# S5 preparation on GpSimd, its products on VectorE, and another order of the first block's stages

## The chip, the cores and the metric

The kernel runs on one core of one Trainium2 chip. Within the core TensorE (PE) multiplies matrices, VectorE (DVE), ScalarE (ACT) and GpSimd (POOL) work on tiles in SBUF and PSUM, and SyncE (SP) issues most of the loads. The metric is the device time of one execution in microseconds; lower is better.

## The reference

A first block (a mixer of two branches with a gate each, cross attention and a convolutional feed-forward layer) is followed by a second network of two further layers, on 256 tokens of 1024 channels. The change lies in the mixer of the first block:

```python
h = _rmsnorm(x, mix_norm_g[l])
u_s5, q_in, k_in, v_in, o_in, i_pre, f_pre, gate_pre = jnp.split(h @ w_in[l], split_points, axis=-1)
y_s5 = _s5(u_s5, ...)
y_m = _mlstm(q_in, k_in, v_in, o_in, i_pre, f_pre, ...)
g_s5, g_m = jnp.split(sigmoid(gate_pre + b_gate[l]), 2, axis=-1)
merged = g_s5 * (y_s5 @ w_br_s5[l]) + g_m * (y_m @ w_br_m[l])
x = x + merged @ w_out[l]
```

`_s5` is a linear recurrence with complex states, in 32 groups of 64 states and 16 channels:

```python
a_bar = jnp.exp(lam * dt)                       # dt = exp(log_dt)
b_bar = ((a_bar - 1.0) / lam)[..., None] * b_mat
_, states = lax.associative_scan(combine, (a_seq, bu), axis=1)
y = einsum(states, c_mat).real + d * u;  y = gelu(y);  y = y * sigmoid(y @ w_glu + b_glu)
```

`_mlstm` has a convolution of 4 taps over q and k (with SiLU), four heads with exponential gates over two chunks of 128 tokens, and a norm over each head.

## The kernel before

**Matrix products.** Weights come as fp32 tiles of 128 x 1024 (one DMA each, on SP) and are split into a high part (`hi`, L320, on ACT) and a rest (`lo`, L321, on DVE); `wload` makes both, and three matmuls (L328 to L330, or L337 to L339 with the tokens as rows) make one product step, with `xh` and `xl` the two parts of the activations. Three `hi` and three `lo` tiles exist in this block, so ACT and DVE run at most three weights ahead of PE. Two tiles of 128 x 1024 give one PSUM tile `g` of 128 x 512 (48 matmuls), called a pair below; `g` has three buffers, the smaller products (`a`) four.

**Order.** The program's text gives priorities (`high_priority`, and the order of writing), and the scheduler of the Tile framework sets each engine's own list from them by a simulated timeline. On the chip each engine works through its list strictly in order and waits at an instruction whose input isn't there.

**The first block's stages** as written: the S5 preparation `s5_prep`; the norm (`rms_defer`: squares, column sums at L454, the reciprocal root `rmsr` as a power on POOL at L505, a broadcast by PE at L498); `u` (two pairs, evacuated at L1637); `s5`, which makes everything from powers to the S5 output; `qk` (four pairs, each with its convolution `ev_qk`: a product with the token scale at L1646, six taps on DVE at L1654, and L1657); `vif`, `vm` and `o` (tokens as rows); `mlstm`; the eight gate pairs (L1696, L1698); `s5_glu`; the two branch products `w_brs` and `w_brm`; and the output projection `w_out`, where the block's mixer ends.

**S5 preparation.** `s5_prep` computes a_bar, its powers 0 to 4 (`pr`, `pi`), the input factors (`cr`, `ci`) and the scan factors (`akr`, `aki`, `akn`) from tiles of 128 x 16, in some hundred small instructions on DVE (a sine and cosine by polynomials among them); POOL computes two powers of e, `s5dt` and `s5er`. It has a high priority.

**S5 products.** For each of four blocks of four groups, `outer` multiplies factors and matrices: B on DVE (`mb`, 128 x 256, L747, then written into block diagonal form in two halves of the partitions, L759 and L762), C on POOL (`mc`, 128 x 320, L747, then L765 and L768 into `CR` and `CN`). PE transposes the B blocks (L772) and multiplies B with C (L777, L779) into the short kernel `KS`.

**State and scan.** 32 small matmuls (L795) make the chunk inputs, ACT copies them into `ST` (L796), and `combine` runs over `ST` ten times, five instructions each (L806 to L810). The S5 output (L830) multiplies `U`, `KS`, `ST`, `CR` and `CN`.

**mLSTM.** The gates' part (L859 to L899) is a chain of tiny instructions; each of four heads then does L905 on PE, `arg` (L908, DVE), exponentials on ACT, the scores (L914, L915), `pT` (L917, DVE), the sums (L919 to L921) and `hs` (L927, DVE). A norm over all heads follows (`rstd_cols`, a power on POOL), with `hn` (L937), a transposition (L938) and the branch's input.

Of the kernel before, what the change touches and what calls it, by code (L numbers as in the profile page):

```python
# [13 lines left out]
F32R = mybir.dt.float32r  # L14
# [6 lines left out]
P = 128  # L21
# [106 lines left out]
def host_arrays(i):  # L128
# [67 lines left out]
    pe_.add("lr", gp(g["s5_lam_re"][0]))  # L196
    pe_.add("li", gp(g["s5_lam_im"][0]))
# [61 lines left out]
def _program(ctx, tc, nc, a, offs, dump):  # L259
# [42 lines left out]
    def pexp(x, shape, tag):  # L302
# [5 lines left out]
        ts(c, x, ECOR, 1.0, op0=mult, op1=add)  # L308
        tt(r, r, c, op=mult)
        return r  # L310
# [328 lines left out]
    def s5_prep(bp):  # L639
        t16 = lambda tag, n=16: T(bp, [P, n], tag)  # L640
        lr, li, ldt = C["lr"], C["li"], C["ldt"]
        dt = pexp(ldt, [P, 16], "s5dt")
        xr, th = t16("xr"), t16("th")
        tt(xr, lr, dt, op=mult)
        tt(th, li, dt, op=mult)
        er = pexp(xr, [P, 16], "s5er")
# [10 lines left out]
        z, sn, cn, w = t16("z"), t16("sn"), t16("cn"), t16("w")  # L657
# [4 lines left out]
        stt(sn, sn, 1.0, r, op0=mult, op1=mult)  # L662
# [7 lines left out]
        j, cq, sq = t16("j"), t16("cq"), t16("sq")  # L670
        rnd(j, n, 0.25)
        stt(j, j, -4.0, n, op0=mult, op1=add)
        stt(w, j, -1.0, j, op0=mult, op1=ALU.max)
# [3 lines left out]
        pr = T(bp, [P, 16, 5], "pr")  # L677
        pi = T(bp, [P, 16, 5], "pi")
        G.memset(pr[:, :, 0:1], 1.0)
        G.memset(pi[:, :, 0:1], 0.0)  # L680
        ar, ai = pr[:, :, 1], pi[:, :, 1]

        def cmul(orr, oi, xr_, xi_, yr, yi):
            n_ = len(orr.shape) > 2 and orr.shape[2] or 1
            sh = list(orr.shape)
            t = [T(bp, sh, "cm%d_%d" % (n_, q_), bufs=2) for q_ in range(4)]
            tt(t[0], xr_, yr, op=mult)
            tt(t[1], xi_, yi, op=mult)
            tt(t[2], xr_, yi, op=mult)
            tt(t[3], xi_, yr, op=mult)  # L690
            tt(orr, t[0], t[1], op=sub)
            tt(oi, t[2], t[3], op=add)

        cs_, sn_ = t16("cs_"), t16("sn_")
        cmul(cs_, sn_, cn, sn, cq, sq)
        tt(ar, er, cs_, op=mult)
        tt(ai, er, sn_, op=mult)
        den, a1 = t16("den"), t16("a1")
        tt(den, lr, lr, op=mult)
        tt(z, li, li, op=mult)  # L700
        tt(den, den, z, op=add)
        V.reciprocal(den, den)
        nli = t16("nli")
        ts(nli, li, -1.0, None, op0=mult)
# [12 lines left out]
        akr, aki, akn = T(bp, [P, NL, 16], "akr"), T(bp, [P, NL, 16], "aki"), T(bp, [P, NL, 16], "akn")
        V.tensor_copy(akr[:, 0, :], pr[:, :, 4])
        V.tensor_copy(aki[:, 0, :], pi[:, :, 4])
        for k in range(1, NL):  # L720
            cmul(akr[:, k, :], aki[:, k, :], akr[:, k - 1, :], aki[:, k - 1, :], akr[:, k - 1, :], aki[:, k - 1, :])
        ts(akn, aki, -1.0, None, op0=mult)
        return cr, ci, pr, pi, akr, aki, akn

    def s5(bp, b2, K5, U, prep):
        cr, ci, pr, pi, akr, aki, akn = prep
        NL = 5
# [14 lines left out]
        def outer(eng, xa, ya, xb, yb, nt, tag):  # L742
            sh = [P, 4, nt, 16]
            m = []
            for x_, y_ in ((xa, ya), (xb, yb)):
                t = T(bp, sh, tag + str(len(m)))
                eng.tensor_tensor(t, bc(x_[:, :, :, None], sh), bc(y_[:, :, None, :], sh), op=mult)  # L747
                m.append(t)
            return m

        halves = [(g, slice(64 * g, 64 * g + 64)) for g in range(2)]
        for b in range(4):
            s4 = slice(4 * b, 4 * b + 4)
            BR, BI = bt[b % 2][:, 0], bt[b % 2][:, 1]
# [1045 lines left out]
```

## Time and profile before

| what | value |
|---|---|
| time, median of three runs | 1218.49 us (1217.42 to 1223.27) |
| the profiled execution | 1222.49 us, of which the span is 1220.7 |
| PE busy | 1175.4 us (96%) |
| DVE busy | 905.4 us (74%) |
| ACT busy | 681.7 us (56%) |
| POOL busy | 94.5 us (8%) |
| mean granted PE clock | 0.98 |

Busy shares are means over stages with different limits. A windows view gives each engine's busy time in a stretch, and PE's granted clock there (1.00 is 2.4 GHz, 0.50 is 1.2 GHz); a timeline gives each instruction's start and duration, and in square brackets how long its engine was idle before it and what ended that.

### The profile page before, as it was taken

What the parts mean: (1) busy time and instruction counts of PE and PEld (TensorE: products, weight loads), DVE (VectorE), ACT (ScalarE), POOL (GpSimd) and SP (SyncE); (2) the same over time, 40 slices, a digit from 0 to 9 for tenths busy, and PEclk for the clock granted to TensorE, in tenths of its full rate; (3) what the DMA queues carried; (4) which work ended last, traced back from release to release, by engine and by line L of the source; (5) the groups of instructions that cost most, each with busy time, mean ns of one, the idle gap of its engine ahead of it and who ended that gap; (6) DMA issues with size and microseconds to landing.
All of it is one profiled execution on the core that took longest, in us unless ns stands there. A gap on an engine that the chain in (4) does not pass through costs nothing.

```text
span 1220.7 us, 23603 instructions
## 1 busy us (share of the span) xinstructions
PE 1175.4 (96%) x9370; PEld 1111.6 (91%) x9370; DVE 905.4 (74%) x1744; ACT 681.7 (56%) x1205; POOL 94.5 (8%) x94
## 2 busy tenths in 40 slices
PE   7779999999999999999999899999999999999997
PEld 7769989999999999899998899998977789999986
DVE  8998957866689886667564886666687758976654
ACT  5345564755566765446355675554675566755541
POOL 4830000100000000000001000001000001000010
PEclk9979999999999999999999899999998999999998
DMA  7423445664356556656423556566754215666561
GB/s 262 139 87 114 147 137 179 205 202 157 100 177 196 183 177 181 196 175 215 163 79 106 170 173 187 176 181 190 261 182 139 70 54 193 208 188 188 160 201 36
DMA packets 61276, 199.41 MB, mean 163 GB/s; under 512 B 8502, under 2 KB 12398, under 8 KB 60910
## 3 DMA queue, kind: packets, MB, share of 16 engines
q1 hardware_dynamic: 54864, 191.60, 49.5%
q10 hardware_dynamic: 6302, 6.32, 1.6%
q8 instruction: 73, 1.20, 0.4%
q14 instruction: 37, 0.30, 0.1%
HBM read 196.28 MB, written 1.60 MB: 162 GB/s over the span
## 4 chain that ended last, share of the span: by engine, by line
PE 82%; DVE 11%; ACT 2%; DMA 2%; issue 2%; SPq 0%; DVEq 0%; ACTq 0%
PE g L329 10%; PE g L328 10%; PE g L330 10%; PE a L328 7%; PE a L329 7%; PE a L330 7%; PE a L393 5%; PE g L393 4%; DVE lo L321 3%; PE a L395 3%; PE g L337 2%; PE g L339 2%; PE g L338 2%; PE g L395 2%; PE a L947 1%
## 5 line engine op out<-in xcount | busy, mean ns | idle before, releaser
L321 DVE TENSOR_TENSOR lo<-raw,hi 128x1024 fp32r<-128x1024 f32 (+3 forms) x359 | 431.2, 1206 | 180.7 <-ACT hi L320 178.0
L320 ACT CAST hi<-raw 128x1024 fp32r<-128x1024 f32 (+3 forms) x359 | 363.7, 1020 | 355.4 <-PE g L329 138.8
L328 PE MATMUL g<-xh,hi 128*128 128x256 f32 (+1 forms) x616 | 176.2, 287 | 7.9 <-ACT xh L568 7.6
L329 PE MATMUL g<-xl,hi 128*128 128x256 f32 (+1 forms) x624 | 178.9, 287 | 0.3 <-DVE xl L569 0.3
L330 PE MATMUL g<-xh,lo 128*128 128x256 f32 (+1 forms) x616 | 176.3, 287 | 2.7 <-DVE lo L321 2.7
L328 PE MATMUL a<-nh,hi 128*128 128x256 f32 x560 | 159.9, 286 | 4.6 <-ACT sqa L1061 2.7
L329 PE MATMUL a<-nl,hi 128*128 128x256 f32 x560 | 159.5, 285 | 0.9 <-DVE nl L516 0.9
L330 PE MATMUL a<-nh,lo 128*128 128x256 f32 x560 | 159.3, 285 | 0.0
L328 PEld LDWEIGHTS g<-xh,hi 128*128 128x128 f32 x616 | 117.7, 191 | 9.9 <-ACT xh L568 7.9
L330 PEld LDWEIGHTS g<-xh,lo 128*128 128x128 f32 x616 | 117.4, 191 | 4.4 <-DVE lo L321 3.4
L329 PEld LDWEIGHTS g<-xl,hi 128*128 128x128 f32 x624 | 119.0, 191 | 1.4 <-DVE xl L569 0.9
L328 PEld LDWEIGHTS a<-nh,hi 128*128 128x128 f32 x560 | 108.6, 194 | 5.7 <-ACT sqa L1061 2.9
L329 PEld LDWEIGHTS a<-nl,hi 128*128 128x128 f32 x560 | 108.7, 194 | 1.1 <-DVE nl L516 1.1
L330 PEld LDWEIGHTS a<-nh,lo 128*128 128x128 f32 x560 | 108.7, 194 | 0.0
L393 PE MATMUL a<-mx,hi 128*128 128x512 f32 x264 | 91.9, 394 | 0.0
L328 PE MATMUL g<-nh,hi 128*128 128x256 f32 x288 | 81.5, 283 | 0.0
L329 PE MATMUL g<-nl,hi 128*128 128x256 f32 x288 | 81.5, 283 | 0.0
L330 PE MATMUL g<-nh,lo 128*128 128x256 f32 x288 | 81.5, 283 | 0.0
L395 PE MATMUL a<-mx,lo 128*128 128x256 f32 x264 | 73.1, 277 | 0.0
L393 PE MATMUL g<-mx,hi 128*128 128x512 f32 x198 | 69.0, 395 | 0.0
L393 PEld LDWEIGHTS a<-mx,hi 128*128 128x128 f32 x264 | 49.4, 188 | 11.5
L328 PEld LDWEIGHTS g<-nh,hi 128*128 128x128 f32 x288 | 55.3, 192 | 0.0
(619 smaller groups left out, 2905.2 us busy)
## 6 DMA issues: line engine op xcount, KB each, us to landing
raw<-g_up SPq DMA_DIRECT2D x88, 512.0 KB, 3.6
raw<-f_up SPq DMA_DIRECT2D x44, 512.0 KB, 3.5
raw<-g_dn SPq DMA_DIRECT2D x32, 512.0 KB, 3.6
raw<-w_fm SPq DMA_DIRECT2D x27, 512.0 KB, 4.1
raw<-ev_fm SPq DMA_DIRECT2D x20, 512.0 KB, 3.7
raw<-f_dn SPq DMA_DIRECT2D x16, 512.0 KB, 3.6
raw<-od_fm SPq DMA_DIRECT2D x14, 512.0 KB, 4.2
raw<-g_dn SPq DMA_DIRECT2D x16, 384.0 KB, 3.4
```

Of the source, the lines that this page charges most:

```text
L320: ACT.copy(hi, raw)
L321: tt(lo, raw, hi, op=sub)
L328: mm(ps, hi[:, o:o + P], xh[:, k, :], start=start and k == 0, stop=False, skip_group_check=skip)
L329: mm(ps, hi[:, o:o + P], xl[:, k, :], start=False, stop=False, skip_group_check=skip)
L330: mm(ps, lo[:, o:o + P], xh[:, k, :], start=False, stop=stop and k == kt - 1, skip_group_check=skip)
L337: mm(ps, xh[:, k, t], hi[:, wsl], start=start and j == 0, stop=False, skip_group_check=skip)
L338: mm(ps, xh[:, k, t], lo[:, wsl], start=False, stop=False, skip_group_check=skip)
L339: mm(ps, xl[:, k, t], hi[:, wsl], start=False, stop=stop and j == len(ks) - 1, skip_group_check=skip)
L393: mm(f2, hi[:, o], X[:, k].rearrange("p a s -> p (a s)"), start=first and j == 0, stop=False, skip_group_check=True)
L395: mm(ps[:, 0, :], lo[:, o], X[:, k, 0, :], start=False, stop=last and j == len(ks) - 1, skip_group_check=True)
L947: PE.transpose(tr[:, k, :], b, ident)
```

## The change

1. **Preparation on POOL.** `s5_prep` runs on GpSimd but for three instructions, with real and imaginary parts packed in one tile (`pz`, `cz`, `ak`, `ax`), and each multiply-add of DVE split in two. It has no priority of its own any more and is written after `u`.
2. **Products on DVE.** `inputs(b)` handles eight groups at a time, in two blocks; each of its four outer products is three DVE instructions of 128 x 640 or 128 x 512 (L760, L761 in the numbering of the changed kernel), and ACT writes all block diagonals. The combine of the scan has four instructions, not five.
3. **Order.** u, gates 0 and 1, `inputs(0)`, gates 2 and 3, vif, `inputs(1)`, vm, the mLSTM gates, the state, o, qk, the scan, the heads, gates 4 to 7, the S5 output, the m branch, the sigmoid's product, the S5 branch with the merge.
4. The zero tiles are made elsewhere (`s5_zero`: the block diagonals' on DVE, `KS` and `CN` on POOL), and some buffers are shared with others.

```diff
     def s5_prep(bp):
+        tt, ts = G.tensor_tensor, G.tensor_scalar
...
+        def stt(o, x_, c, y_, op0, op1):
+            ts(s_, x_, c, None, op0=op0)
+            tt(o, s_, y_, op=op1)
...
-        dt = pexp(ldt, [P, 16], "s5dt")
...
+        dt = pexp(ldt, [P, 16], "s5dt", G)
+        xt = t2("xt")
+        tt(xt, ll, bc(dt[:, None, :], [P, 2, 16]), op=mult)
...
+        def cmul(o, x_, y_, conj=False):
...
+            tt(u, x_, y_, op=mult)
+            tt(v, x_, y_[:, ::-1], op=mult)
...
+                tt(o[:, 0], u[:, 0], u[:, 1], op=sub)
+                tt(o[:, 1], v[:, 0], v[:, 1], op=add)
...
-            m = outer(V, crb, brb, cib, bib, 4, "mb")
...
-            c = outer(G, prb, xrb, pib, xib, 5, "mc")
...
+        def outer(xa, ya, xb, yb, nt, op):
+            sh = [P, 8, nt, 16]
+            m = [T(bp, sh, "so", bufs=2), T(bp, sh, "hs")]
+            for t, x_, y_ in ((m[0], xa, ya), (m[1], xb, yb)):
+                tt(t, bc(x_[:, :, :, None], sh), bc(y_[:, :, None, :], sh), op=mult)
+            tt(m[0], m[0], m[1], op=op)
+            return m[0]
+
+        def inputs(b):
...
+            m = outer(pr, xr, pi, xi, 5, sub)
             for g, hs in halves:
+                ACT.copy(CR[hs, s8, :, g, :], m[hs])
...
-            tt(t1, src, bc(akr[:, k, :][:, None, :, None], [P, 2, 16, n_]), op=mult)
-            tt(t2[:, 0], src[:, 1], ak(aki), op=mult)
-            tt(t2[:, 1], src[:, 0], ak(akn), op=mult)
+            tt(t1, src, bc(ak[:, k, 0][:, None, :, None], sh), op=mult)
+            tt(t2, src[:, ::-1], bc(ax[:, k][:, :, :, None], sh), op=mult)
...
-        with tc.high_priority(500):
-            prep = s5_prep(bp)
+        zero = s5_zero(bp)
...
         gemm_pairs("w_fm", range(2), 8, xh, xl, ev_u, ahead=ahead)
-        y5 = s5(bp, b2, K5, U, prep)
+        prep = s5_prep(bp)
+        s5_inputs, s5_state, s5_scan, s5_output = s5_steps(bp, K5, U, prep, zero)
...
+        gates([0, 1])
+        s5_inputs(0)
+        gates([2, 3])
...
+        gemm_tm("w_vif", range(1), xh, xl, ev_vif, cw=264)
+        s5_inputs(1)
+        gemm_tm("w_tm", range(1, 2), xh, xl, ev_vm)
+        mg = mlstm_gates(bp, K5, ifs)
+        s5_state()
+        gemm_tm("w_tm", range(2, 4), xh, xl, ev_o)
...
         gemm_pairs("w_fm", range(2, 6), 8, xh, xl, ev_qk)
...
+        s5_scan()
+        ymh, yml = mlstm(bp, b2, K5, mg, qk, vm, og)
+        gates([4, 5, 6, 7])
+        gs, gm = gate
+        y5 = s5_output()
...
+        gemm_pairs("w_brm", range(4), 4, ymh, yml, ev_bm, cw=256)
         ysh, ysl = s5_glu(bp, b2, y5)
...
         gemm_pairs("w_brs", range(4), 4, ysh, ysl, ev_bs, cw=256)
```

Line numbers of the changed kernel are one less than before's up to L640 (`lo` is L320, the matmuls L327 to L329, rmsr L504), and others behind.

On POOL, before, at the start of the program: the two powers (`s5dt`, `s5er`), a sum of squares, the reciprocal root, and the first C products.

```order
L306 TENSOR_TENSOR s5dt_122<-ebase_96,early_104 128x16
L473 TENSOR_TENSOR sqa_328<-sq_318,sq_320 128x512
L306 TENSOR_TENSOR s5er_131<-ebase_96,xr_127 128x16
L505 TENSOR_TENSOR rmsr_339<-rmsms_337,mhalf_94 128x2
L747 TENSOR_TENSOR mc_117_491<-pr_169,cs_80_297 128x320
L747 TENSOR_TENSOR mc_118_493<-pi_170,cs_80_297 128x320
```

The same place now (`cs` the sine and cosine, `st` a scratch tile, `z` the square of the angle):

```order
L644 TENSOR_SCALAR st_305<-cs_330 128x16
L645 TENSOR_TENSOR cs_330<-st_305,z_328 128x16
L672 TENSOR_TENSOR cs_330<-cs_330,r_319 128x16
L644 TENSOR_SCALAR st_305<-cs_330 128x16
L504 TENSOR_TENSOR rmsr_177<-rmsms_175,mhalf_94 128x2
L673 TENSOR_TENSOR cs_330<-cs_330,r_319 128x16
L645 TENSOR_TENSOR cs_330<-st_305,z_328 128x16
L677 TENSOR_TENSOR cs_330<-cs_330,z_328 128x16
```

The reciprocal root `rmsr` stood right behind `s5er`; now 21 rows of the preparation stand between, and 42 more between it and the last row that writes `pz`.

On DVE, before, around the third `lo` tile of vif (128x528), which PE waits for; `akr`, `aki` are scan factors, `w` a block of B, `mcv` the convolution:

```order
L1654 SCALAR_TENSOR_TENSOR mcv_1137<-msg_1135,consts_91,mcv_1137 128x254
L691 TENSOR_TENSOR akr_250<-cm_0_72_275,cm_1_73_276 128x16
L692 TENSOR_TENSOR aki_251<-cm_2_74_277,cm_3_75_278 128x16
L1654 SCALAR_TENSOR_TENSOR mcv_1137<-msg_1135,consts_91,mcv_1137 128x253
L321 TENSOR_TENSOR lo_1360<-raw_1357,hi_1359 128x528
L762 SCALAR_TENSOR_TENSOR w_112_473<-mb_126_534,mb_127_536 64x16x16 x2
```

On DVE now, where the first products stand (`so`, `hs` product tiles, `cs_19` the packed B and C matrices, `mcv` here a gate pair, L1672):

```order
L320 TENSOR_TENSOR lo_541<-raw_538,hi_540 128x1024
L1672 TENSOR_TENSOR mcv_503<-g_442,rs_182 128x512
L760 TENSOR_TENSOR so_572<-pz_358,cs_19_135 128x640
L760 TENSOR_TENSOR so_579<-pz_358,cs_19_135 128x640
L760 TENSOR_TENSOR hs_573<-pz_358,cs_19_135 128x640
L320 TENSOR_TENSOR lo_658<-raw_655,hi_657 128x1024
L761 TENSOR_TENSOR so_572<-so_572,hs_573 128x640
L320 TENSOR_TENSOR lo_688<-raw_685,hi_687 128x1024
```

Three products that read `pz` stand ahead of `lo_658`, a weight of the gates' third pair; before, scan factors, convolution taps and B products stood around `lo_1360`.

On DVE, before, in the scan, its second combine:

```order
L810 TENSOR_TENSOR ST_682<-ST_682,w_165_725 128x32x32
L321 TENSOR_TENSOR lo_1819<-raw_1816,hi_1818 128x1024
L806 TENSOR_TENSOR w_166_731<-ST_682,akr_250 128x32x16
L807 TENSOR_TENSOR w_167_732<-ST_682,aki_251 128x16x16
L808 TENSOR_TENSOR w_167_732<-ST_682,akn_252 128x16x16
L878 COPY bcum_1604<-m_1600 128x8
L321 TENSOR_TENSOR lo_1854<-raw_1851,hi_1853 128x1024
L1684 TENSOR_SCALAR og_1301<-og_1301 128x256
L809 TENSOR_TENSOR ST_682<-ST_682,w_166_731 128x32x16
```

On DVE now, the same combine (L821 to L824; `msg`, `mcv` at L1718 and L1726 are the convolution of a q/k pair):

```order
L320 TENSOR_TENSOR lo_1354<-raw_1351,hi_1353 128x1024
L1718 TENSOR_TENSOR msg_1306<-g_1245,rs_182 128x512
L821 TENSOR_TENSOR w_255_1552<-ST_127,ak_408 128x32x16
L822 TENSOR_TENSOR w_256_1553<-ST_127,ax_409 128x32x16
L932 TENSOR_TENSOR arg_1610<-a_1608,cs_19_135 128x2x128
L320 TENSOR_TENSOR lo_1399<-raw_1396,hi_1398 128x1024
L823 TENSOR_TENSOR ST_127<-ST_127,w_255_1552 128x32x16
L1726 SCALAR_TENSOR_TENSOR mcv_1308<-msg_1306,consts_91,mcv_1308 128x255 x2
L320 TENSOR_TENSOR lo_1429<-raw_1426,hi_1428 128x1024
L824 TENSOR_TENSOR ST_127<-ST_127,w_256_1553 128x32x16
L1726 SCALAR_TENSOR_TENSOR mcv_1308<-msg_1306,consts_91,mcv_1308 128x254 x2
```

Between the scan's instructions stood `lo` tiles, the output gate and the mLSTM's gate chain; now stand `lo` tiles, a head's `arg` and the taps of the q/k convolutions, all four of which lie between the first and the last instruction of the scan.

## Rows read from the trace of the kernel before

**Rows 1.** Window of 40 us: PE, PEld, DVE, ACT, POOL busy us (x count), PEclk, DMA share, GB/s

```profile
40.00:80.00 40.00, 26.02 (x169) 22.71 (x168) 37.96 (x65) 12.90 (x25) 29.91 (x30) 0.79 0.22 70
```

**Rows 2.** Windows of 5 us, first block; same columns

```profile
65.00:70.00 5.00, 1.08 (x5) 1.08 (x5) 4.99 (x7) 0.00 (x0) 4.71 (x6) 0.50 0.03 6
...
85.00:90.00 5.00, 5.00 (x45) 5.00 (x44) 4.50 (x12) 3.29 (x5) 1.68 (x1) 1.00 0.65 195
```

**Rows 3.** Timeline of PE, 54 to 80 us (start, duration, instruction, idle before)

```profile
68.92 0.59 PE L338 MATMUL g<-lo,xh 128*128 128x264 f32 x1 [6.83 <-DVE lo L321]
```

**Rows 4.** Timeline of POOL, 0 to 80 us

```profile
23.24 0.69 POOL L505 TENSOR_TENSOR rmsr<-rmsms,mhalf 128x2 f32<-128x2 f32 x1 [7.82 <-ACT rmsms L503]
35.15 2.17 POOL L747 TENSOR_TENSOR mc<-pr,cs 128x320 f32<-128x320 f32 x1 [11.21 <-DVE pr L691]
...
41.58 0.80 POOL L747 TENSOR_TENSOR mc<-pr,cs 128x320 f32<-128x320 f32 x1
```

**Rows 5.** Timeline of POOL, small operations in later blocks

```profile
871.06 0.19 POOL L1038 TENSOR_TENSOR lnv<-lnmu 128x2 f32<-128x2 f32 x1 [3.47 <-ACT lnmq L1036]
871.34 0.20 POOL L1039 TENSOR_TENSOR lnv<-lnmq,lnv 128x2 f32<-128x2 f32 x1
...
1026.24 1.05 POOL L1050 TENSOR_TENSOR lnn<-lnmu,lnr 128x2 f32<-128x2 f32 x1
```

**Rows 6.** Timeline of DVE, 80 to 90 us: a convolution step and a lo

```profile
83.20 0.48 DVE L1654 SCALAR_TENSOR_TENSOR mcv<-msg,consts,mcv 128x254 f32<-128x254 f32 x1
83.60 1.22 DVE L321 TENSOR_TENSOR lo<-raw,hi 128x1024 fp32r<-128x1024 f32 x1
84.73 0.48 DVE L1654 SCALAR_TENSOR_TENSOR mcv<-msg,consts,mcv 128x254 f32<-128x254 f32 x1
```

**Rows 7.** Timeline of DVE, 102 to 152 us: the scan

```profile
102.64 1.23 DVE L806 TENSOR_TENSOR w<-ST,akr 128x1024 f32<-128x1024 f32 x1 [2.63 <-ACT ST L796]
103.79 0.68 DVE L807 TENSOR_TENSOR w<-ST,aki 128x512 f32<-128x512 f32 x1
104.39 0.69 DVE L808 TENSOR_TENSOR w<-ST,akn 128x512 f32<-128x512 f32 x1
...
127.62 0.18 DVE L808 TENSOR_TENSOR w<-ST,akn 128x16 f32<-128x16 f32 x1
...
149.57 1.19 DVE L810 TENSOR_TENSOR ST<-ST,w 128x992 f32<-128x992 f32 x1
```

**Rows 8.** Timeline of PE, from the S5 output to the output projection

```profile
152.84 0.30 PE L830 MATMUL a<-U,KS 128*32 128x64 f32 x8
152.96 0.30 PE L830 MATMUL a<-ST,CR 128*32 128x64 f32 x8
...
173.34 1.02 PE L424 MATMUL g<-w,raw 128*128 128x256 f32 x4
...
180.60 0.48 PE L328 MATMUL g<-KS,hi 128*128 128x256 f32 x2
...
192.54 0.28 PE L328 MATMUL g<-CR,hi 128*128 128x256 f32 x1
...
203.74 0.28 PE L328 MATMUL g<-xh,hi 128*128 128x256 f32 x1
```

**Rows 9.** Timeline of PE, 94 to 103 us: state matmuls, first and last

```profile
94.63 1.10 PE L795 MATMUL a<-U,gs 128*128 128x64 f32 x8
...
101.92 0.43 PE L830 MATMUL a<-U,KS 128*32 128x64 f32 x16
```

**Rows 10.** Timeline of DVE, 159 to 172 us: last head and norm

```profile
160.26 0.42 DVE L908 TENSOR_TENSOR arg<-a,cs 128x256 f32<-128x256 f32 x1
...
166.28 0.61 DVE L927 SCALAR_TENSOR_TENSOR hs<-a,mrd,og 128x128 f32<-128x128 f32 x2
...
169.78 0.48 DVE L937 TENSOR_SCALAR hn<-hs,mlsr 128x128 f32<-128x128 f32 x2
```

**Rows 11.** Windows of 4 us in the odd block; columns as in rows 1

```profile
908.00:912.00 4.00, 1.81 (x8) 1.26 (x7) 3.88 (x14) 3.92 (x11) 0.00 (x0) 0.72 0.43 114
912.00:916.00 4.00, 4.00 (x18) 2.74 (x18) 2.20 (x15) 3.33 (x13) 0.71 (x1) 0.50 0.47 149
...
920.00:924.00 4.00, 4.00 (x29) 1.86 (x21) 3.84 (x17) 3.68 (x12) 0.00 (x0) 0.57 0.77 221
```

**Rows 12.** Timeline of PE, 25 to 29 us: the reader of rmsr

```profile
26.28 0.61 PE L498 MATMUL m<-consts,rmsr 128*128 128x128 f32 x4
```

More of the change, by code (lines that the diff above doesn't have):

```diff
@@ L676, in s5_prep @@
         tt(sq, sq, j, op=mult)
[L677 to L692, printed above, removed]
@@ new lines, in s5_prep @@
+        G.memset(pz[:, 0, :, 0:1], 1.0)
+        G.memset(pz[:, 1, :, 0:1], 0.0)
+        def cmul(o, x_, y_, conj=False):
+            sh = list(o.shape)
+            n_ = len(sh) > 3 and sh[3] or 1
+            u, v = [T(bp, sh, "cm%d_%d" % (n_, q_), bufs=2 if n_ == 1 else 1) for q_ in range(2)]
+            tt(u, x_, y_, op=mult)
+            tt(v, x_, y_[:, ::-1], op=mult)
+            if conj:
+                tt(o[:, 0], u[:, 0], u[:, 1], op=add)
+                tt(o[:, 1], v[:, 1], v[:, 0], op=sub)
+            else:
+                tt(o[:, 0], u[:, 0], u[:, 1], op=sub)
+                tt(o[:, 1], v[:, 0], v[:, 1], op=add)
@@ L791, in s5 @@
-        for b in range(4):
-            vp = T(pa, [P, 2, 4, 64], "a")
-            for r_, W in enumerate((VR, VI)):
-                for q in range(4):
-                    mm(vp[:, r_, q, :], W[:, 4 * b + q, :], U2[:, 4 * b + q, :], start=True, stop=True)
-            ACT.copy(ST[:, :, 4 * b:4 * b + 4, 1:], vp)
+                ACT.copy(CN[hs, s8, :, g, :], m[hs])
+            for r_, ops in enumerate(((cr, br, ci, bi, 4, sub), (cr, bi, ci, br, 4, add))):
+                m = outer(*ops)
+                for q in range(2):
+                    for g, hs in halves:
+                        act(bt[q][hs, r_, :, :, g, :], m[hs, 4 * q:4 * q + 4], AF.Copy, scale=1.0 - 2 * r_)
@@ new lines, in s5_steps, with state @@
+        box = {}
+        def state():
+            us = T(dr, [16, 32, 4, 64], "us")
+            U2 = box["U2"] = T(bp, [P, 16, 64], "U2")
+            nc.scalar.dma_start(us.rearrange("(a j) q t c -> (j q) a (t c)", a=4),
+                                U.rearrange("p a t c -> p a (t c)"))
+            for t in range(4):
+                nc.scalar.dma_start(U2[32 * t:32 * t + 32], us.rearrange("a q t c -> t q a c")[t])
+            for b in range(4):
+                vp = T(pa, [P, 2, 4, 64], "a")
+                for r_, W in enumerate((VR, VI)):
+                    for q in range(4):
+                        mm(vp[:, r_, q, :], W[:, 4 * b + q, :], U2[:, 4 * b + q, :], start=True, stop=True)
+                ACT.copy(ST[:, :, 4 * b:4 * b + 4, 1:], vp)
@@ L835, in s5, with scan, output @@
-        dump("s5y", y)
-        return y
+        def scan():
+            for k in range(NL):
+                combine(k, 2 << k, 64 >> (k + 1))
+            for k in range(NL - 1, -1, -1):
+                n_ = (64 >> (k + 1)) - 1
+                if n_:
+                    combine(k, 3 << k, n_)
+        def output():
+            U2 = box["U2"]
+            y = T(bp, [P, 4, S], "w40")
+            Y4 = T(bp, [P, 4, 4, 64], "w41")
+            for b in range(2):
+                yp = T(pa, [P, 2, 4, 64], "a")
+                for k in range(2 * b, 2 * b + 2):
+                    for t in range(4):
+                        for step in range(3):
+                            for j in range(4):
+                                jj = 4 * k + j
+                                w = (KS[:, jj, 32 * t:32 * t + 32] if step == 0
+                                     else (CR, CN)[step - 1][:, jj, t + 1].rearrange("p g h -> p (g h)"))
+                                v = U2[:, jj, :] if step == 0 else ST[:, step - 1, jj, 0:64]
+                                mm(yp[32 * j:32 * j + 32, k % 2, t, :], w, v, start=step == 0, stop=step == 2,
+                                   skip_group_check=True)
+                    Y = Y4[:, k]
+                    stt(Y, U[:, k], C["s5_d"][:, k:k + 1], yp[:, k % 2], op0=mult, op1=add)
+                    act(y[:, k, :].rearrange("p (c t) -> p t c", t=4), Y, AF.Gelu_apprx_tanh)
+            dump("s5y", y)
+            return y
@@ L838, in s5_glu @@
+        return inputs, state, scan, output
     def s5_glu(bp, b2, y):
```

273 lines of the change are left out of this document (117 added, 156 removed).

## The prediction

> **What bounds the kernel now.** I read the windows of 40 us first. The poor stretch of the first block is 40 to 80, where TensorE (PE) ran 169 matmuls in 40 us at a mean granted clock of 0.79, with VectorE (DVE) busy for 37.96 of the 40 [rows 1]. The windows of 5 us size the loss: an undisturbed one holds 45 matmuls, so 40 us hold 360, and 191 are missing; at the 0.119 us that one 128x256 step takes (96 of them from 180.60 to 192.54, and 96 from 192.54 to 203.74, give 0.124 and 0.117 [rows 8]) that is some 20 us. While PE starved, the clock fell to the lower of its two levels (0.50, 1.2 GHz) [rows 2]. The releaser names the cause: the longest wait of PE there, 6.83 us, was for a lo tile of DVE [rows 3]. DVE is the engine whose queue is full there, and GpSimd (POOL) slows it or is slowed: the same 128x320 product takes POOL 2.17 us beside DVE and 0.80 without it [rows 4]. So the first block, which ends where the output projection starts (203.74 [rows 8]), is where a change can act; of the rest of the program only two tiles' worth of order differs, and I price that at nothing.
>
> **The sum is made on the time of the first output-projection matmul**, 203.74 us of a profiled execution that took 1222.49 in all. What is gained or lost there I add to the median of the runs, 1218.49.
>
> **Start: the reciprocal root behind the small operations.** On POOL the row rmsr, which ran from 23.24 to 23.93 [rows 4], now stands behind 21 small operations of the preparation, and the PE row that reads it (26.28 in before [rows 12]) comes 36 rows sooner in the program: 26.28 - 36 x 0.119 = 22.0. What rmsr gains by sums that come sooner, the 21 operations take (21 x 0.20 to 0.27 = 4.2 to 5.7 us, prices below, from the end of the second power, 15.4 in before and a little sooner now, and one or two DVE lo tiles between): 21 to 24.5. I keep 23.9 for its end; PE then waits 1.9 us, with the ends 0 and 2.5.
>
> **When is the preparation done?** Call that T. Behind rmsr stand 42 more small POOL operations until pz and cz, the powers, are complete (ahead of the products). POOL's price for a small operation: 0.20 by duration, 0.27 from start to start when one needs the other, and 1.05 when a lo of DVE is running [rows 5]; DVE takes 0.18 for one of 128x16 [rows 7], and overlaps one with the next. 42 operations at 0.24 are 10.1 us, and three lo tiles of 1.13 [rows 6] that hold POOL up add 3.4: T = 23.9 + 13.5 = 37.4. The ends: 42 x 0.20 with nothing held up gives 32.3, 42 x 0.27 with four lo gives 39.8. I take 37, near the upper end since DVE has lo tiles at hand all that time. The Trainium skill (SBUF — State Buffer, "Who interferes with whom") says that a DVE instruction with two SBUF inputs and a GpSimd instruction that reads SBUF exclude each other for the whole instruction. The 1.05 of [rows 5] agrees. The same skill (GPSIMD Engine Reference, "Engine selection") puts elementwise work on VectorE, GpSimd being about 2x slower; that rule speaks against this move, and here it is 0.20 to 0.27 against 0.18 or less.
>
> **Behind T.** DVE's queue is strict: three 128x640 products that need pz stand ahead of the lo tile that PE needs for the gates' third pair. Such a product costs 0.73 (between a 128x512 at 0.60 and a 128x1024 at 1.15 [rows 7]); three and the lo are 3.4, with the semaphores 3.7. PE comes there 118 matmuls after the reader of rmsr, at 23.9 + 14.0 = 37.9, but goes on at T + 3.7 = 40.7: 2.8 us of stall. From there PE's own list to the end of the state matmuls is 228 matmuls of 128x256 at 0.119 (27.1), 48 of 264 columns (5.9), 32 transposes at 0.11 (3.5), 64 records for the state (94.63 to 101.92, 7.3 or 0.114 each [rows 9]) and 64 as small for the K matrix (7.1), small ones 0.9: 51.8, and 2 us for waits on blocks. The scan on DVE can start one ACT copy (0.8) later, at T + 58.3 = 95.3. Before it started at 102.64 [rows 7]. **Gain: 7.3 us**; that is what is left of the 20.
>
> **The scan stretch becomes DVE's.** In before, first to last scan instruction took 102.64 to 150.76 = 48.1 us without idle time [rows 7], and the four q/k convolutions had been done before it, in the 40-to-80 hole and its sides. Now all four stand between the scan's instructions. DVE's rows from the first to the last scan instruction, added up: 17 lo at 1.13 (19.2); the scan 24.7 (25.3 before, one instruction of five folded into another in each of ten steps, so that little is saved); four convolutions, each 0.60 + 6 x 0.40 + 0.60 = 3.6 [rows 6] (14.4); four gate products at 0.60 (2.4); the heads' small ones 2.1. Sum 62.8, against 48.1: **loss 14.7 us**. PE's list beside it is 394 matmuls and one and a half heads, 49.7 us, so PE waits about 13 us there, spread over PSUM buffers that a late multiplication has not freed (5 us), the first head's scores behind the second q/k pair (5.5) and the second head (3.2). The scan ends at 95.3 + 62.8 = 158.1, before 150.76.
>
> **The tail.** In before the gates' matmuls lie between the heads, and hide them: from the last scan instruction to the output projection are 53.0 us. Now the last gate matmul is ahead of the heads' second half, and PE has only 18 matmuls to put between them. One head costs from arg to hs some 6.6 us in before (160.26 to 166.89), and hn follows 2.9 us later [rows 10]; two heads, partly over each other, and the norm are 15.5 us. Behind that lie the S5 output (384 records, eight in 0.11 [rows 8], 5.3, and 1 for its blocks' change), 78 matmuls of the first branch (9.3), the sigmoid's product (7.26, 173.34 to 180.60), 1 us for its split and the other branch (12.0) [rows 8]: 35.9. 51.4 against 53.0: **gain 1.6**, although PE idles 10 us in it, since all gate matmuls are then done, of which some lay behind the scan before. Sum so far: -7.3 + 14.7 - 1.6 = **+5.8**.
>
> **The clock.** In the odd block a PE busy 1.81 of 4 us, at 908 to 912, was followed by a granted clock of 0.50 with PE busy throughout, and so on at 0.57 in the window of 920 to 924 [rows 11]. In the changed kernel there are two such places, the stall of 2.8 us at T and the 15 us of heads with little between. In [rows 11] the 12 us at half rate cost some 6 us of matmul time; a short stall may cost nothing. I take half of what one drop costs, 3, for the tail, and nothing to 3, say 0.5, at T, where PE was full just before. **+3.5.** Total +9.3: 1218.49 + 9.3 = 1228.
>
> **Rivals.** (a) *The hole decides, faster.* The 20 us between 40 and 80 are the one large loss, and they go. It asks that T is 32 (POOL never held up), that the first stall is then 0, that the scan starts at 92 (37.9 + 53.8 + 0.8), and that the heads run over each other within 8 us, not 15.5, and that no clock drop follows. Then 92 + 62.8 + 8 + 35.9 = 198.7, -5; with a scan stretch less full than my sum by 5 us it is -10: 1208 to 1213, the greater part beyond 0.5%. For it: DVE's preparation was slowed by POOL itself (DVE was busy for nearly all of 40 to 80 [rows 1], and POOL's product of 0.80 took 2.17 beside it [rows 4]), a loss that the move ends. Against: the prices in the 62.8 are of rows that POOL didn't touch. (b) *POOL is held up throughout, much slower.* If each small operation meets a busy port at 0.7 (between the 0.20 and 1.05 of [rows 5]), 42 are 29 us, T = 53, the first block ends 16 us later than at T = 37: 1244. It decides from T above 45. For it: the 2.17 against 0.80 of [rows 4]. Against: DVE waits for pz itself and soon has nothing to run. (c) *Stall for stall.* T of 32 to 36 and no clock drop at either place: 92 + 62.8 + 51.4 = 206, +2.5: 1221, no change that can be measured. (d) That the engines' order differs from the text of the change: excluded, since the order of instructions shows each move; it is part of no sum.
>
> **How the numbers follow.** Forecast 0.44 (1228, its own range 1223 to 1234), (a) 0.20, (b) 0.12, (c) 0.24. A run of this kernel can tell about 0.5% (6.1 us) from no change. Slower by more than that: (b) and 0.38 of the forecast: 0.50. Faster by more: 0.18 of (a). Within: the rest of these two, 0.08, and (c): 0.32. The range leaves out the far half of (a) and of (b): 1210 to 1240.
>
> **What would show it.** Right: rmsr later than PE's need, a PE wait of 1.5 to 3 us near 21; the last power on POOL near 37 and a PE wait for lo right behind it; the first scan instruction at 93 to 98 and the last at 156 to 161 with DVE idle near 0 between; PE at 0.5 to 0.7 busy share in the stretch of the last two heads; output projection at 206 to 216. Wrong: POOL's small operations at 0.15 or less (T below 31), the scan's end before 152, or heads that end within 8 us of it. If the output projection starts as forecast and the total doesn't move with it, the rest of the program isn't the same as I took it to be.

## The result and the profile after

The changed kernel takes **1229.68 us** (median, 1227.53 to 1233.91) against 1218.36 (1216.95 to 1223.27) before: a ratio of **1.0096, 95% interval 1.0075 to 1.0116**. It is slower by 11.3 us, as forecast (1228). The profiled execution took 1227.53, its span 1225.7. In it the output projection starts at 214.18 instead of 203.74 [rows 8], 10.4 us later. Behind that point little more shows: the rest took 1011.5 us here and 1017.0 in the profiled execution of before, which itself was 4.1 us above its kernel's median. The first 1300 matmuls of the rest took 159.8 us here and 158.5 in before, so that difference arises later, in code that the change doesn't touch. Nearly all of the loss, as far as the profiles show it, arises in the first block.

Windows of the changed kernel (PE, PEld, DVE, ACT, POOL busy us with counts, granted clock of PE, DMA share, GB/s):

```profile
40.00:80.00 40.00, 38.58 (x318) 36.97 (x319) 33.49 (x58) 36.25 (x67) 13.39 (x18) 1.00 0.46 147
80.00:120.00 40.00, 39.97 (x334) 39.04 (x332) 29.46 (x49) 17.69 (x28) 1.64 (x1) 1.00 0.38 122
120.00:160.00 40.00, 30.57 (x220) 28.62 (x220) 39.86 (x78) 19.55 (x37) 0.00 (x0) 0.95 0.44 139
160.00:200.00 40.00, 31.86 (x529) 28.47 (x530) 17.35 (x38) 14.74 (x35) 1.64 (x1) 0.80 0.15 46
...
155.00:160.00 5.00, 2.38 (x12) 1.71 (x12) 4.96 (x12) 2.43 (x10) 0.00 (x0) 0.93 0.60 197
160.00:165.00 5.00, 3.82 (x11) 2.77 (x12) 2.10 (x8) 2.30 (x13) 0.00 (x0) 0.50 0.06 25
165.00:170.00 5.00, 2.22 (x9) 1.63 (x7) 1.49 (x5) 1.56 (x8) 0.00 (x0) 0.50 0.00 0
170.00:175.00 5.00, 2.53 (x11) 2.21 (x12) 2.34 (x8) 0.98 (x3) 1.64 (x1) 0.50 0.00 0
```

The hole of [rows 1] is gone: 318 matmuls where 169 ran, at full clock. What PE lost moved to 120 to 200: first VectorE is full (39.86 of 40), then nobody is, and the clock is at its lower level. The longest waits of PE in the first 225 us (total, times, longest); the first is the wait for the input at the program's start, 7.6 us in before:

```profile
PE g L327 <- ACT xh L567: 8.0, 1, 8.0
PE a L943 <- DVE pT L941: 5.4, 3, 3.5
PE a L962 <- DVE hn L961: 4.5, 2, 4.3
PE g L329 <- DVE lo L320: 3.8, 2, 3.0
PE g L327 <- DVE ST L823: 3.0, 1, 3.0
PE g L327 <- DVE msg L1718: 2.4, 2, 1.6
PE m L497 <- POOL rmsr L504: 2.1, 1, 2.1
PE a L848 <- issue: 1.7, 1, 1.7
```

The wait of 6.83 us for a lo [rows 3] has become 3.0; the others are new or grew: the heads (`pT`, `hn`), a scan instruction that stands ahead of what PE needs (`ST`), a convolution (`msg`), the reciprocal root (`rmsr`).

The start, in timelines of POOL, DVE and PE:

```profile
22.55 0.72 POOL L504 TENSOR_TENSOR rmsr<-rmsms,mhalf 128x2 f32<-128x2 f32 x1
23.72 1.08 POOL L677 TENSOR_TENSOR cs<-cs,z 128x16 f32<-128x16 f32 x1
27.94 1.29 POOL L645 TENSOR_TENSOR w<-st,w 128x16 f32<-128x16 f32 x1
37.62 0.25 POOL L703 TENSOR_TENSOR pz<-cm 128x32 f32<-128x32 f32 x1
```

```profile
37.70 1.63 DVE L760 TENSOR_TENSOR so<-pz,cs 128x640 f32<-128x640 f32 x2 [4.70 <-POOL pz L702]
40.03 1.27 DVE L320 TENSOR_TENSOR lo<-raw,hi 128x1024 fp32r<-128x1024 f32 x1
95.72 1.23 DVE L821 TENSOR_TENSOR w<-ST,ak 128x1024 f32<-128x1024 f32 x1 [2.03 <-ACT ST L812]
157.41 1.22 DVE L824 TENSOR_TENSOR ST<-ST,w 128x992 f32<-128x992 f32 x1
171.78 0.48 DVE L961 TENSOR_SCALAR hn<-hs,mlsr 128x128 f32<-128x128 f32 x2 [2.52 <-POOL mlsr L504]
```

```profile
23.33 0.71 PE L497 MATMUL m<-consts,rmsr 128*128 128x128 f32 x4 [2.11 <-POOL rmsr L504]
41.36 0.39 PE L329 MATMUL g<-xh,lo 128*128 128x256 f32 x1 [3.03 <-DVE lo L320]
172.21 0.66 PE L962 MATMUL a<-consts,hn 128*128 128x128 f32 x2 [4.26 <-DVE hn L961]
214.18 0.28 PE L327 MATMUL g<-xh,hi 128*128 128x256 f32 x1
```

The chain can be read off: GpSimd works until 37.87, VectorE idles 4.70 us for it, its three products then stand ahead of the lo for which PE waits. The scan's rows run from 95.72 to 158.63, 62.9 us (48.1 in [rows 7]).

### The profile page after: what moved, and what is told of

It reads as the page before. It is cut to its first block, busy times and chain, and to the rows that moved or that the text cites. A ratio compares the mean times of both kernels' runs of the same rounds, so it can differ in the third digit from the quotient of the medians.

```text
span 1225.7 us, 23565 instructions
## 1 busy us (share of the span) xinstructions
PE 1173.9 (96%) x9370; PEld 1109.7 (91%) x9370; DVE 883.8 (72%) x1628; ACT 691.9 (56%) x1227; POOL 92.7 (8%) x145
## 4 chain that ended last, share of the span: by engine, by line
PE 84%; DVE 8%; ACT 3%; issue 2%; DMA 2%; POOL 1%; ACTq 0%; SPq 0%; DVEq 0%
PE g L328 11%; PE g L327 11%; PE g L329 11%; PE a L327 7%; PE a L328 7%; PE a L329 7%; PE a L392 5%; PE g L392 4%; PE a L394 2%; DVE lo L320 2%; PE g L338 2%; PE g L336 2%; PE g L337 2%; PE g L394 2%; PE a L971 1%
## 5 line engine op out<-in xcount | busy, mean ns | idle before, releaser
L320 DVE TENSOR_TENSOR lo<-raw,hi 128x1024 fp32r<-128x1024 f32 (+3 forms) x359 | 428.4, 1198 | 182.4 <-ACT hi L319 179.6
L327 PE MATMUL g<-xh,hi 128*128 128x256 f32 (+1 forms) x616 | 176.0, 286 | 13.8 <-ACT xh L567 8.0
L329 PE MATMUL g<-xh,lo 128*128 128x256 f32 (+1 forms) x616 | 175.7, 286 | 4.2 <-DVE lo L320 4.2
L327 PE MATMUL a<-nh,hi 128*128 128x256 f32 x560 | 159.8, 286 | 4.2 <-ACT sqa L1085 2.8
L329 PE MATMUL a<-nh,lo 128*128 128x256 f32 x560 | 159.0, 284 | 0.0
L327 PEld LDWEIGHTS g<-xh,hi 128*128 128x128 f32 x616 | 117.8, 191 | 15.9 <-ACT xh L567 8.2
L329 PEld LDWEIGHTS g<-xh,lo 128*128 128x128 f32 x616 | 117.4, 191 | 5.5 <-DVE lo L320 4.9
L327 PEld LDWEIGHTS a<-nh,hi 128*128 128x128 f32 x560 | 108.5, 194 | 5.2 <-ACT sqa L1085 2.9
L329 PEld LDWEIGHTS a<-nh,lo 128*128 128x128 f32 x560 | 108.4, 194 | 0.0
L327 PE MATMUL g<-nh,hi 128*128 128x256 f32 x288 | 81.5, 283 | 0.0
L329 PE MATMUL g<-nh,lo 128*128 128x256 f32 x288 | 81.5, 283 | 0.0
L327 PEld LDWEIGHTS g<-nh,hi 128*128 128x128 f32 x288 | 55.3, 192 | 0.0
```

Of the source, the lines that this page charges most:

```text
L320: tt(lo, raw, hi, op=sub)
L327: mm(ps, hi[:, o:o + P], xh[:, k, :], start=start and k == 0, stop=False, skip_group_check=skip)
L329: mm(ps, lo[:, o:o + P], xh[:, k, :], start=False, stop=stop and k == kt - 1, skip_group_check=skip)
```

## The experiments

Two columns size every kernel: when the scan starts on VectorE (preparation and products lie ahead of it), and how long it is from there to the output projection (order and tail). The third is what follows the start of the output projection in the profiled execution. It is one execution's: five kernels that share the two things which turn out below to move it (a list of ScalarE and the place of the tiles) took 1011.5 to 1017.0, so differences of some 5 us in this column say nothing.

| kernel | time, median us | scan starts | from there to output projection | rest |
|---|---|---|---|---|
| before | 1218.4 | 102.6 | 101.1 | 1017.0 |
| changed | 1229.7 | 95.7 | 118.5 | 1011.5 |
| order alone | 1238.1 | 102.3 | 121.4 | 1012.2 |
| no taps | 1222.3 | 95.0 | 102.2 | 1022.3 |
| q/k early | 1216.0 | 100.7 | 99.6 | 1013.8 |
| preparation on VectorE | 1232.3 | 87.9 | 120.1 | 1024.7 |
| the same, mem later | 1215.5 | 88.4 | 119.5 | 1004.1 |
| root first | 1234.4 | 92.0 | 120.3 | 1019.9 |
| VectorE and q/k early | 1212.3 | 98.4 | 98.8 | 1012.6 |

My theory was the prediction's: the new preparation and products win some 7 us at the start of the scan, and the q/k convolutions, which now share VectorE with the scan, lose more behind it. The first rival: the parts cost (a GpSimd preparation on the path), and the order is harmless.

**Order alone.** The old preparation (on VectorE, with its priority), the old products (C on GpSimd) and the old combine under the new order; the edit's core:

```diff
-        prep = s5_prep(bp)
+        with tc.high_priority(500):
+            prep = s5_prep(bp)
...
+            c = outer(G, prb, xrb, pib, xib, 5, "mc")
```

> The new order alone: preparation on DVE with high priority, four blocks with C products on POOL and B products on DVE, five-instruction combine, all as before the change; the stages in the changed order. Theory A (the order makes the loss, preparation and products move little): the hole at 40 to 80 is smaller than before, since 12 us of convolutions leave it, the scan starts at 92 to 99 and lasts 62 to 65, output projection at 210 to 218, total 1225 to 1233. Theory B (preparation and products make the loss): total 1214 to 1221.

1238.06 us, ratio 1.0157 (1.0138 to 1.0177), slower even than I expected. The hole stays, as the window and the longest wait show: taking the convolutions out of the first 100 us did not bring the scan forward (102.3, where I expected 92 to 99; 102.6 in before), and why isn't shown. The stretch behind the scan's start is somewhat longer than in the changed kernel (121.4 against 118.5):

```profile
40.00:80.00 40.00, 26.70 (x197) 24.27 (x195) 38.69 (x64) 16.18 (x30) 29.19 (x30) 0.91 0.28 87
...
PE g L337 <- DVE lo L320: 5.9, 1, 5.9
...
223.68 0.28 PE L327 MATMUL g<-xh,hi 128*128 128x256 f32 x1
```

The rival falls: the order costs 20 us at the output projection (223.68 against 203.74), and preparation, products and combine together gain back 9.5.

**No taps.** The changed kernel without the 24 multiply-adds of the q/k convolution (of its four taps one is left; the kernel leaves the other three out):

```diff
-                for d in range(1, 4):
-                    stt(y[:, d:], hv[:, n, :S - d], cw[:, 3 - d:4 - d], y[:, d:], op0=mult, op1=add)
```

> The changed kernel without the three taps per half that DVE adds in each q/k convolution (24 instructions; that part of the convolution is left out). A price by itself. Theory A (the scan stretch is DVE's sum): 24 x 0.39 = 9.4 us fall out of 62.9, the scan ends 9 to 10 us sooner (148 to 150 instead of 158.6), output projection at 203 to 207, total 1218 to 1222. Theory B or C (the stretch is bound by PE, or by the clock): scan end and total move by less than 3 us, total 1226 to 1231.

From the scan's start to the output projection it takes 102.2 us instead of 118.5: without the taps nearly all of the excess over before (101.1) is gone, and the output projection starts sooner than I expected (203 to 207):

```profile
94.97 1.23 DVE L821 TENSOR_TENSOR w<-ST,ak 128x1024 f32<-128x1024 f32 x1 [2.02 <-ACT ST L812]
145.12 1.19 DVE L824 TENSOR_TENSOR ST<-ST,w 128x992 f32<-128x992 f32 x1
197.21 0.28 PE L327 MATMUL g<-xh,hi 128*128 128x256 f32 x1
```

The 24 taps of 0.40 us are 9.6 us of VectorE, and 16.3 us are saved: 11.6 in the scan's stretch (51.3 instead of 62.9) and 4.7 behind it. I have not separated the other 6.7: the lists differ (14 `lo` tiles stand in the stretch instead of 17), and less time is spent below full clock (the windows of 4 us from 136 to 144 and from 156 to 180 in the changed kernel, only those from 152 to 160 here). The time, 1222.28, ratio 1.0033 (1.0016 to 1.0050), is just above what I expected, for a reason that lies behind the first block: see "mem later".

**q/k early.** The four q/k pairs stand where the first gates stood, and all gates behind the scan (so `VR` moves into the gates' first buffer, which is free until then); preparation and products are the changed ones:

```diff
-        gates([0, 1])
+        qks([2, 3])
         s5_inputs(0)
-        gates([2, 3])
+        qks([4, 5])
...
-        gates([4, 5, 6, 7])
+        gates(list(range(8)))
```

> Of the changed kernel the preparation on POOL and the products on DVE stay; only the order of matmul stages changes: the four q/k pairs stand where the first four gate pairs and the late q/k pairs stood (two before the first products, two behind), and all eight gate pairs come after the scan is started. Theory A (the loss is the order: four convolutions, 14.4 us of DVE, were put between the scan's instructions, and the gate matmuls that could fill PE beside the heads were spent early): the convolutions run in DVE's idle time at 65 to 95, first scan instruction at 96 to 101, scan stretch 62.9 - 14.4 + 1 = 49 to 52, no clock drop beside the heads, first output-projection matmul at 198 to 204 where the changed kernel has 214.2; total 1212 to 1220. Theory B (the loss is the late preparation on POOL): still there, so no gain: output projection at 211 to 217, total 1226 to 1233.

1215.99 us, ratio 0.9981 (0.9968 to 0.9993): the loss is gone. The scan starts 5 us later than in the changed kernel, behind the convolutions, which VectorE now runs from 41.8 to 84.8. But its rows take 45.3 us, not 62.9, and PE has gate matmuls to run between the heads, at full clock. The edit moves convolutions and gates at once; what each gives is not separated.

```profile
100.71 1.23 DVE L821 TENSOR_TENSOR w<-ST,ak 128x1024 f32<-128x1024 f32 x1 [2.70 <-ACT ST L812]
144.83 1.17 DVE L824 TENSOR_TENSOR ST<-ST,w 128x992 f32<-128x992 f32 x1
200.30 0.28 PE L327 MATMUL g<-xh,hi 128*128 128x256 f32 x1
...
120.00:160.00 40.00, 40.00 (x326) 38.99 (x326) 37.62 (x70) 23.15 (x51) 1.84 (x1) 1.00 0.50 158
160.00:200.00 40.00, 37.56 (x617) 35.47 (x616) 22.03 (x32) 18.19 (x25) 0.00 (x0) 1.00 0.39 123
```

**Preparation on VectorE.** The changed kernel, its preparation on VectorE with the priority that it had before:

```diff
-            ts(s_, x_, c, None, op0=op0)
-            tt(o, s_, y_, op=op1)
...
-        prep = s5_prep(bp)
+        with tc.high_priority(500):
+            prep = s5_prep(bp)
```

> The changed kernel with its preparation on DVE again (packed tiles, multiply-adds in one instruction, high priority; POOL keeps the two powers); products, blocks and order as changed. Theory A: both early PE waits (2.1 us for the reciprocal root, 3.0 for the lo behind the products) go, the scan starts some 5 us sooner, at 90 to 93 instead of 95.7, its stretch stays 61 to 64, output projection at 208 to 211, total 1223 to 1227: part of the loss only. Theory B (the preparation on POOL is what costs): total 1216 to 1220, as before the change. Rival C (DVE is so full that it needs POOL's help): the scan starts at 96 or later, total 1229 or more.

The output projection starts at 207.98, 6.2 us sooner than in the changed kernel and about where theory A puts it, but the way there was another. The scan starts at 87.88, sooner than A says, and its rows take 53.2 us, not 61 to 64, since 18 of the 24 taps and 14 `lo` stand among them. What that gains is lost behind the last of them: from there to the output projection it takes 66.9 us, 55.6 in the changed kernel, so that scan's start and output projection lie as far apart as there (120.1 and 118.5). PE waits for the convolutions' first product and for what they give to the heads:

```profile
87.88 1.23 DVE L817 TENSOR_TENSOR w<-ST,ak 128x1024 f32<-128x1024 f32 x1 [2.48 <-ACT ST L808]
...
PE g L327 <- DVE msg L1715: 5.1, 3, 3.0
PE a L934 <- DVE x L1726: 4.2, 1, 4.2
...
207.98 0.28 PE L327 MATMUL g<-xh,hi 128*128 128x256 f32 x1
```

So it is the new products (with the packed form of preparation and combine) that gain, 14.4 us at the scan's start against order alone, and giving the preparation to GpSimd takes 7.8 of that back. The engine, the priority and the splitting of the multiply-adds are put back together here, and not separated. The Trainium skill (GPSIMD Engine Reference, "Engine selection") gives elementwise work to VectorE; these 7.8 us agree in direction. But the total, 1232.25, missed: the rest took 1024.7. ScalarE's timeline shows a wait there, and PE's what it cost:

```profile
219.13 3.31 ACT L567 ACTIVATE oh<-mem,consts 128x256 fp32r<-128x256 f32 x8 [2.99 <-DMA mem<-mem]
```

```profile
225.60 0.58 PE L327 MATMUL g<-xh,hi 128*128 128x256 f32 x1 [4.18 <-ACT hi L319]
```

In this kernel's ScalarE list the cross attention's preparation of `mem` stands two `hi` casts earlier than in before and the changed kernel (behind 50 of them, not 52); its transfer hasn't landed, and the casts that PE needs are queued behind the wait.

**The same, mem later.** To test that, `mem` is multiplied in place by ones that depend on the first result of the output projection, so that the list has its preparation two casts later:

```diff
+        one8 = T(tp, [P, 8], "one8")
+        G.tensor_copy(one8, x1[:, 0, 0:8])
+        G.memset(one8, 1.0)
...
+        G.tensor_tensor(mem[:, :, 0], mem[:, :, 0], one8, op=mult)
```

> The changed kernel with its preparation back on VectorE, as the run before that took 1232.3 us with the output projection at 207.98, and one thing more: the cross attention's activations are multiplied in place by ones that depend on the first result of the output projection, 256 elements on a line of their own on GpSimd, so that ScalarE takes up their preparation two high parts later in its list, where it stands in the kernel before and in the changed one. Theory A (the 1020 to 1025 us behind the output projection, where the others take 1011.5 to 1014, come from these two places in ScalarE's list: it waits there for the transfer of mem with a weight's high part queued behind): ScalarE's wait for mem of 3.0 us and TensorE's wait of 4.2 us for hi near 225 go, the rest of the program takes 1011 to 1015, the time is 1219 to 1224. Rival B (it is another thing in that list, or a clock drop that follows from the first block): the wait may go, the rest stays at 1019 to 1025 and the time at 1229 to 1234. The output projection starts at 207 to 209 in both.

The wait is gone, the output projection stays at 207.99, and 1300 matmuls later PE is at 158.2 us from there, against 166.8 without the edit, 159.8 in the changed kernel and 158.5 in before. So the two places in that list cost 8.6 us. But the time, 1215.48, ratio 0.9983 (0.9967 to 0.9999), was better than theory A: the rest took 1004.1, less than in any kernel so far. The matmuls on `nh` and `nl` (in later stages) follow each other in 116.3 ns instead of 120.0; the new tile moves the tiles behind it.

**An unused tile.** That tile alone, in three kernels, and one of twice its size in the third:

```diff
+        pad = T(tp, [P, 8], "pad")
+        G.memset(pad, 1.0)
```

> The changed kernel with one unused tile of 128x8 (two buffers) more in a pool that lies ahead of the later stages' tiles, so that these lie 64 bytes further in each partition; the lists stay (one memset on GpSimd and a pair of neighbouring rows apart). In the run before this one, whose extra tile had that size, the matmuls on nh and nl (1,680 of form a, 864 of form g) went from 120.0 ns start to start to 116.2, in all other kernels 120.0. Theory A (the place of the tiles sets that): 116.2 ns here too, 2544 x 3.8 ns = 9.7 us less, some 1 us more on mx; the rest of the program 1003 to 1006 us, the time 1220 to 1223, with the output projection at 213 to 215 as in the changed kernel. Rival B (it was the other list of that kernel): 120.0 ns, 1228 to 1232.

> The kernel with the preparation on VectorE and early q/k pairs (1212.3 us), with the same unused tile. Theory A (the place of the tiles sets the matmuls' pace on nh): output projection at 196 to 199 as there, the rest 1003 to 1006, the time 1202 to 1205. Rival B: no difference, 1210 to 1214.

> The kernel before with the same unused tile of 128x8 in two buffers, nothing else changed but one memset on GpSimd. Theory A (the place of the later stages' tiles alone sets the pace of the matmuls on nh, 116.2 ns instead of 120.0 as in two kernels that have the extra tile): 116.2 here too, the first block as before (output projection 203 to 205), 1209 to 1212. Rival B (the pace hangs on the tiles of the changed kernel, whose pools differ): 120.0 ns and 1216 to 1221. By A the change, the order and the place of the tiles are three separate terms, and the change of this case (1229.7 against 1218.4, both at 120.0 ns) isn't touched by it.

> The fastest kernel so far (1203.0 us) with an unused tile of 128x16 instead, so that the later tiles lie 128 bytes further instead of 64. Theory A1 (any shift from the place of before gives 116.2 ns): 1202 to 1205. Theory A2 (what matters is whether the shift is an odd number of 64 bytes): 120.0 ns as without the tile and 1210 to 1214.

| kernel | without | tile of 64 bytes (two buffers of 32) | tile of 128 bytes |
|---|---|---|---|
| before | 1218.4, 120.0 ns | 1210.2, 116.2 ns | |
| changed | 1229.7, 120.0 ns | 1221.5, 116.3 ns | |
| VectorE and q/k early | 1212.3, 120.0 ns | 1203.0, 116.0 ns | 1212.7, 119.1 ns |

The ns are means from start to start over the nh and nl matmuls; the bytes are worked out from the tile's size, the addresses themselves were not read. The window of 10 us, of the changed kernel and of the one with the tile, shows it in counts at the same full clock:

```profile
1100.00:1110.00 10.00, 10.00 (x85) 10.00 (x85) 6.62 (x11) 6.26 (x10) 0.00 (x0) 1.00 0.59 175
```

```profile
1100.00:1110.00 10.00, 10.00 (x90) 10.00 (x89) 7.13 (x12) 5.52 (x9) 0.00 (x0) 1.00 0.59 196
```

Where the tiles lie sets that pace, 7 to 9 us of the whole. The 128 bytes gave a pace of their own (neither of the two that I had expected), so I can't say which property of the address it is. Before and changed both have 120.0: this is no part of their difference, and with the tile they differ by the same 11 us.

**VectorE and q/k early.** Both edits together:

> Preparation on VectorE at high priority and the products of the change, and the q/k pairs early, the gates behind the scan. Theory A (the change's two new parts pull apart: preparation and products gain, the late q/k convolutions lose; and the GpSimd preparation's 63 small operations cost 6 us of the start, since with the preparation on VectorE the output projection started 6.2 us sooner, 207.98 against 214.18): the output projection starts at 194 to 198, from the 200.3 that early q/k pairs gave with the preparation on GpSimd; the time is 1208 to 1214, below the kernel before (1218.4) and below 1216.0. Rival B (with q/k early, VectorE is full in the first 80 us with the convolutions, so that a preparation there delays them by its own some 10 us, and GpSimd was the better place in that order): output projection at 200 to 206, 1216 to 1222. Rival C (the start gains as A says, but the list of ScalarE for the cross attention behind it again puts a transfer that hasn't landed ahead of a weight's high part): output projection at 194 to 198 and the time 1216 to 1222, with a wait of ScalarE for the tile mem of over 2 us right behind the output projection.

1212.33, ratio 0.9953 (0.9935 to 0.9971), output projection at 197.27: theory A, though that is 3.0 us sooner than with early q/k pairs alone, not the 6 that it counted on. With the unused tile 1202.96, ratio **0.9870 (0.9850 to 0.9890)**, the fastest here; of its 1.3% against before, 0.5 to 0.8% is the tile's: before gains 0.5% by it (0.9951, 0.9932 to 0.9970), this kernel 0.8% (1202.96 against 1212.33).

**Root first.** The root stands behind 8 instead of 21 small operations of the preparation:

```diff
+        G.tensor_copy(s_[:, 0:2], rc)
```

> The changed kernel with the reciprocal root earlier on GpSimd: it stands behind 8 instead of 21 small operations of the preparation (one tiny copy more makes them wait for the column sums). Theory A (two stalls in series: what ends the first hole is the last power on GpSimd, near 37.9, whatever PE did before): PE's wait for the root, 2.1 us, goes or falls below 0.5, PE comes sooner to the third gate pair and waits there 4.5 to 6 us for lo where it waited 3.0; the scan starts at 95 to 97, the output projection at 213 to 216. Rival B (the two stalls add up, each costs its own): the wait for lo stays at 3.0, scan and output projection 2 us sooner, at 93.6 and 212. The total may differ from 1229.7 by what the lists of the cross attention behind do, so the verdict goes by these two starts.

The wait for the root went (it ended at 19.20, not 23.27). PE still could not pass the stall at the third pair before 41.78 (41.36 in the changed kernel): the preparation ends it, as A says, though its last power came 1.2 us later here (39.09). But the wait for lo was 2.80, not longer, since in that kernel's list some 3 us more of PE's work stands ahead of the stall; the scan started 3.7 us sooner, and of that 1.9 reached the output projection (212.33). Neither theory is shown: the edit moved PE's list too. Its total, 1234.37, carries the wait for mem again (3.1 us on ScalarE, 4.2 on PE).

## Why the prediction was right

- **Root and T.** Forecast 23.9 with a PE wait of 1.9, and T = 37.4 (37 in the sum); measured 23.27 with 2.11, and 37.87. The price per operation held: 0.20 to 0.36 us, with four between rmsr and T held up to 1.08 to 1.29 where I had put three at 1.13 on top. From 33.0 on, with VectorE idle, none was held up.
- **The stall behind T.** 2.8 forecast, 3.0 measured; the scan's start 95.3 against 95.7. That gain of 6.9 is 14.4 from the new products, less the 7.8 that the preparation on GpSimd cost, and 0.3 from the order: my sum held all in one, and two runs separate them.
- **The scan's stretch.** 62.8 forecast as a sum of rows, 62.9 measured, with VectorE busy 62.8 of them; the 17 `lo`, 24 taps and four gate products of the sum all stand in it. That the convolutions make the loss behind the scan's start is shown by the run without the taps, and the one with q/k early agrees. PE idled 8.1 us in it, where I had put about 13. That the output projection moves with this stretch is not so in every list: with the preparation on VectorE it was 9.7 us shorter, and nothing was gained by that.
- **The tail.** 51.4 and 3 for the clock forecast, 55.6 measured. The heads and the norm took 18.8 us from the scan's end to the S5 output, against 15.5; the clock stood at 0.50 from about 159 to 176 while PE ran 9 to 11 matmuls per 5 us. The term was undersized by 1.2 in all. The clock also fell between 136 and 144 (0.85 and 0.72 in windows of 4 us), a third place that I had not seen; VectorE was busy throughout there, so the stretch took no longer than its rows.
- **The clock at T.** 0 to 3, taken as 0.5; it was 0 here (1.00 in the window from 40 to 45). In the same kernel with the unused tile PE's stall was 3.6 us instead of 3.0, the clock was 0.50 there, and the output projection started 2.2 us later (216.34, beyond the 213 to 215 that I expected of that run). Both ends of that bound occur.
- **The rest.** I priced it at nothing. The profiles show no loss there for this change (10.4 of the 11.3 us are in the first block), but it was luck rather than insight: in three of the experiments it took 1019.9 to 1024.7 us, beyond the 1011.5 to 1017.0 of the others at that pace, with a wait for mem in each.
- **Rivals.** (a) failed where I had placed its price: the stretch behind the scan's start was as full as the sum said. (b) failed on T, 37.9 and not above 45. Of the 82 small operations 40 ran with VectorE idle, at 0.20 to 0.36 us each, and 14 beside a VectorE instruction that reads a PSUM tile (`g`) or one tile only, at 0.21 to 0.31; those that were held up all met one with both inputs in SBUF (`lo`, the products). Once VectorE had its products, it was as (b) says: the 19 operations behind T, of 128x16 to 128x80, took 0.75 us in the mean (0.21 to 1.20), but nothing waited for them. (c) failed on both its conditions: T was not 32 to 36, and the clock fell in the tail. One reading was wrong: GpSimd's product of 0.80 [rows 4] did not run without VectorE, which meanwhile ended a block product and ran an operation of 128x16 in 0.59 us, where one takes 0.18 [rows 7]; the pair of rows shows the two engines in each other's way, not GpSimd alone.

## What to carry to other kernels

Add up the rows of the engine that a move loads, from the first to the last instruction of the chain that the move joins: the forecast of 62.8 us came from that sum alone, and decided the sign. Split a large change into an early and a late part by one event on the bounding engine (here the scan's start): the two columns showed at once which part of the change paid for which. And before a total is believed, compare the stretch that the edit does not touch: lists, tiles' places and the scatter of executions moved it by up to 22 us (1002.7 to 1024.7) in kernels whose code there is nearly the same.

## What was not expected of the hardware

- The pace of back-to-back fp32 matmuls (128 x 256) depended on where the operands lie in SBUF: 120.0 ns as placed before, 116.0 to 116.3 with a shift of 64 bytes and 119.1 with one of 128, at a granted clock of 1.00. Others (`mx` with lo) went the other way, 115.9 to 118.4 ns.
- One transfer that is read a few us too early by an engine with a strict queue cost more than its wait: 3.0 us on ScalarE, 4.2 on PE, then a granted clock of 0.54 and 0.78 in the next two windows of 5 us, together 8.6 us.
